# A two-layer hybrid decoder trunk: the compressed branch's probabilities are split ahead of their transposes, and the instruction planner gets other costs and rules

## The chip, the core and the metric

The kernel runs on one core of a Trainium2 chip. The metric is the time of one execution on the device, in microseconds (us). Three executions of the kernel before are recorded: 586.84, 588.35 and 589.41 us, median 588.35. One more execution was taken with the hardware profiler; everything said of single instructions comes from it.

The engines go by short names: PE is the matrix engine (PEld its loading of stationary operands), DVE the vector engine, ACT the scalar engine, POOL the general engine, SP the queue that starts most transfers. Each engine works through its own instructions in the order in which they were written.

## The reference

Two layers, each on x of 512 tokens by 1024 columns in float32. One projection of x by `w_in` (3352 columns) feeds three mixers side by side; their outputs are gated, concatenated, projected by `w_out` and normalised. Cut to what matters here:

```
proj = x @ w_in            # split into rq rk rv rg nq nkc nvc nks nvs nkw nvw ng ngl lx lg
y_ret = retention(rq, rk, rv) * silu(rg)                 # 4 heads of 64, chunks of 128
y_nsa = nsa(nq, nkc, nvc, nks, nvs, nkw, nvw, ngl, ...) * silu(ng)
y_lru = rg_lru(lx, conv_w, conv_b, ...) * silu(lg)       # causal conv of width 4, then a gated recurrence
x = layer_norm(alpha * x + concat(y_ret, y_nsa, y_lru) @ w_out)

# nsa, 8 query heads in 2 groups:
kc = compress(nkc) ; vc = compress(nvc)     # 31 blocks of 32 tokens, stride 16: (block + pos) @ w
p_c = softmax(q kc^T, masked)               # 31 columns          -> o_c = p_c vc
p_s = softmax(q ks^T, causal)               # selected branch     -> o_s   (all 8 blocks fit, so: causal)
p_w = softmax(q kw^T, causal)               # window branch       -> o_w
out = g0 * o_c + g1 * o_s + g2 * o_w        # g = sigmoid(ngl)
```

## The kernel before

Float32 products are built from two parts: a value is split into `hi` (its rounding to the matrix engine's float32r format) and `lo` (the rest), and a product is hi·hi + hi·lo + lo·hi. So every chunk of weights is loaded (`wr`), rounded on ACT (`wh`) and its rest taken on POOL (`wl`), in four pieces of two 256-column slices each; x is kept transposed as `XH` and `XL`. The 13 column chunks of `w_in` are projected in the order of `CHUNKS` (nv, nk, nq0, cmp, nq1, lx, lg, rq, rk, rv, rg, ng0, ng1), then four chunks of `w_out`, for each of the two layers. Products go to eight PSUM banks: three for projections (`A`), two for scores (`S`), one each for transposes (`T`), for values (`O`) and for the rest (`M`).

The attention goes over token tiles of 128 in the order 1, 2, 0, 3 and over two groups of four heads. For a tile, group and branch: the scores in a bank S; DVE adds the mask and finds the maximum (the custom operation that writes `P` and `nmx`); ACT takes the exponential in place and its sum (`den`); `gate_rec` takes the reciprocal of `den` and multiplies by the branch's gate; `scale_row` scales each of the four heads' rows, heads 0 and 1 on POOL and 2 and 3 on DVE (`SCALE = "GGVV"`); in `values`, PE transposes four 128 by 128 blocks into bank T, ACT and DVE split them (`pth`, `ptl`), and two products add to bank O. There are 32 such branch groups and 80 transposed blocks in the two layers.

The compressed branch has 16 small softmaxes (one per tile and group, `pcm`, four heads by 31 columns). Before, `pcm` is transposed as one 128 by 128 block into bank T, and then the transposed block is split: four ACT copies of 32 rows and four DVE subtractions of 32 rows fill 64 rows of `pc` (high parts over low parts), and a product with 64 rows adds to bank O. Bank T is taken until the last of the eight has read it. The compressed keys and values come from `kt2`, which holds the projected columns in its upper 64 rows and the same, one token on, in its lower 64 (DVE copies), and from 16 pairs of products.

The order of the instructions is not the order of the source. Every call is recorded by `Engine.record` and becomes an `Op` with a cost in ns (`Engine.cost`), a lag to its users (`LAG`), a flag whether it holds the SBUF ports that DVE and POOL share (`Engine.locks`), and the buffers that it touches. `Plan.schedule` makes a list schedule: first by the longest path to the end plus a random term (`SEED`, `NOISE`), then six rounds of packing to the end and to the start; the best is written out. Nothing of this runs on the chip: the result is a fixed order per engine and the buffers' places. Line L204 of the profile is the one place where all recorded instructions are issued, and L232 that of the paired products.

Of the kernel before, what the change touches and what calls it, by code (L numbers as in the profile page):

```python
# [17 lines left out]
P = 128  # L18
# [17 lines left out]
# columns of w_in in the order in which they are projected  # L36
# [36 lines left out]
# columns of the table of constants  # L73
C_MASK, C_MASKC, C_ANY, C_COS, C_SIN, C_DQ, C_DQ2, C_DV, C_ID, C_TRI = (
# [37 lines left out]
COLD = 6827.0  # the array's clock is halved until then  # L112
TURN = 130.0  # between two engines' accesses to a bank
# [5 lines left out]
PCB = 1  # L119
# how a token tile's halves are normalised: on DVE; on ACT and DVE; on ACT, DVE and Pool  # L120
NORM = [["AG", "AG", "VV", "VV"], ["AG", "AG", "VV", "VV"]]
LOCKS = True
K_ORDER = [0, 1, 6, 7, 2, 3, 4, 5]
# [3 lines left out]
SCALE = "GGVV"  # L127
W_ENG = "GGGG"
SEED = 174
# [7 lines left out]
class Ref:  # L137
    """A view of a buffer whose place is known once the schedule is."""
# [26 lines left out]
class Slots:  # L165
    """Places of one kind; buffers take them in the order in which they are made."""
# [23 lines left out]
class Engine:  # L190
# [3 lines left out]
    def __getattr__(self, what):  # L194
        f = getattr(self.queue, what)

        def record(*args, **kw):
# [12 lines left out]
            self.plan.add(self.name, call, self.cost(what, args, kw), reads, writes, table, self.locks(what, args, kw))  # L210
# [3 lines left out]
    def locks(self, what, args, kw):  # L214
        """Whether an instruction holds the SBUF ports that DVE and Pool share."""
# [8 lines left out]
        if len(sbuf) > 1:  # L224
            return True
        return what in ("tensor_copy", "tensor_scalar", "memset") and len(sbuf) == len(big) and at(args[0]).space != PSUM

    def together(self, *products):
        """Matrix products that the array takes side by side, as one instruction of the plan."""
# [4 lines left out]
        cost = self.cost("matmul", products[0][:3], {}) + 102.0 * (len(products) - 1)  # L234
        self.plan.add(self.name, call, cost, [r for x in products for r in x[1:3]], [x[0] for x in products], None, False)

    def cost(self, what, args, kw):
        at = lambda x: x.view(0) if isinstance(x, Ref) else x
        size = lambda x: int(np.prod(x.shape[1:]))
        in_psum = lambda x: x.space == PSUM  # L240
        out = at(args[0])
        n = size(out)
        if self.name == "SP":
            return max(475.0, out.nbytes() / DMA_RATE)
        if self.name == "PE":
            if what == "transpose":
                return 0.86 * at(args[1]).shape[0]
# [5 lines left out]
        psum = any(in_psum(x) for x in src)  # L253
        if self.name == "ACT":
            aps = any(isinstance(kw.get(k), Ref) for k in ("bias", "scale"))
            return (52 if psum else 93) + 0.833 * n + 93 * aps + 93 * ("accum_out" in kw)
        n = max([n] + [size(x) for x in src])
        if self.name == "POOL":
            if kw.get("op") == ALU.pow:
                return 164.0 * n  # L260
            if what == "memset":
                return 60 + 0.5 * n
            return 230 + 0.863 * n if what == "tensor_scalar" else 58 + 2.28 * n
        if what == "reciprocal":
            return 60 + 6.3 * n
        if what in ("tensor_copy", "tensor_scalar", "memset") and not psum and not in_psum(out):
            return 67 + 0.521 * n + 62 * (len(src) - 1)
        return 70 + 1.042 * n + 62 * (what == "scalar_tensor_tensor" and len(src) > 2) + (8 if what == "tensor_tensor_reduce" else 0)


class Plan:
# [7 lines left out]
    def touched(self, ref):  # L279
        """The quarters of the partitions and the cells of GRAIN elements that a view touches, as bits."""  # L280
# [15 lines left out]
    def add(self, eng, call, cost, reads, writes, table, lock):  # L296
        op = Op(eng, call, cost, table, lock and LOCKS, len(self.ops))
        for r in reads:
# [12 lines left out]
        op.bufs = {r.buf for r in reads + writes}  # L311
        for b in op.bufs:
# [823 lines left out]
```

## Time and profile before

| | |
|---|---|
| three executions | 586.84, 588.35, 589.41 us |
| span of the profiled execution, first to last instruction | 586.1 us (no time of its own is recorded beside it; the median of the three is 2.2 us more) |
| PE busy | 564.7 us, 96% of the span, 3670 products |
| DVE busy | 415.7 us, 71% |
| ACT busy | 336.7 us, 57% |
| POOL busy | 294.6 us, 50% |
| transfers | 52.6 MB, 90 GB/s over the span |

Busy time is the union of an engine's instructions from start to end. A product's end is modelled and lies well behind the start of the next, so PE can be busy by this count while no new product starts. What matters for PE is the distance from start to start, and what it waited for.

### The profile page before, as it was taken

The page shows a single profiled execution, that of the slowest core. Times are in us where ns is not written, and L with a number is a line of the kernel's source. Part 1 is how long each engine was busy: PE and PEld are TensorE (multiplying, and loading weights), DVE is VectorE, ACT ScalarE, POOL GpSimd, SP SyncE. Part 2 cuts the span into 40 slices and gives each one's busy share as a digit, 9 for nine tenths or more (in the row PEclk, how much of TensorE's full clock was granted, in tenths as well). Part 3 has the DMA queues.
Part 4 walks back from the last instruction along what each step waited for, and adds up shares of the span by engine and source line. Part 5 has one row for each costly group of instructions (what it writes and reads, how often), then busy time and mean ns, then how long its engine had stood idle before and what let it go on. Part 6 is the DMA issues. An engine that isn't in the chain of part 4 may idle for free.

```text
span 586.1 us, 10490 instructions
## 1 busy us (share of the span) xinstructions
PE 564.7 (96%) x3670; PEld 498.3 (85%) x3670; DVE 415.7 (71%) x1237; ACT 336.7 (57%) x785; POOL 294.6 (50%) x349
## 2 busy tenths in 40 slices
PE   8999999999989999999989999999999999999994
PEld 8888867889878888899988888788899888788994
DVE  6663499889998776743793227798797888676247
ACT  6464477698666655722443456758985666564220
POOL 3655155335845255754483454432596514378532
PEclk9999999999999999999999999999999999999997
DMA  8733222110323044343362433120213202332403
GB/s 259 263 100 108 73 72 73 38 36 1 85 61 91 4 124 116 100 148 104 137 180 55 125 79 103 37 73 1 73 38 107 71 21 57 106 127 59 134 7 145
DMA packets 44069, 52.63 MB, mean 90 GB/s; under 512 B 2928, under 2 KB 36720, under 8 KB 44016
## 3 DMA queue, kind: packets, MB, share of 16 engines
q1 hardware_dynamic: 44016, 51.95, 29.8%
q8 instruction: 29, 0.48, 0.3%
q14 instruction: 24, 0.20, 0.1%
HBM read 47.75 MB, written 4.19 MB: 89 GB/s over the span
## 4 chain that ended last, share of the span: by engine, by line
PE 71%; DVE 14%; ACT 8%; issue 2%; DMA 2%; POOL 2%; SPq 0%; DVEq 0%; POOLq 0%; ACTq 0%
PE A L204 50%; PE T L204 6%; PE S L204 6%; PE O L204 4%; PE M L204 4%; DVE P L204 3%; ACT pc L204 2%; DVE pc L204 2%; DVE R L204 2%; ACT P L204 2%; DVE Y L204 2%; DMA wr<-in_w_in_dram 1%; DVE ptl L204 1%; ACT R L204 1%; PE M L232 1%
## 5 line engine op out<-in xcount | busy, mean ns | idle before, releaser
L204 POOL TENSOR_TENSOR wl<-wr,wh 128x512 fp32r<-128x512 f32 (+2 forms) x136 | 180.6, 1343 | 111.5 <-ACT wh L204 93.0
L204 PE MATMUL A<-wh,XL 128*128 128x256 f32 (+1 forms) x560 | 155.3, 288 | 0.7 <-DVE XL L204 0.7
L204 PE MATMUL A<-wh,XH 128*128 128x256 f32 (+1 forms) x560 | 154.1, 288 | 1.1 <-ACT wh L204 1.1
L204 PE MATMUL A<-wl,XH 128*128 128x256 f32 (+1 forms) x560 | 153.6, 285 | 0.0
L204 ACT ACTIVATE wh<-wr 128x512 fp32r<-128x512 f32 (+2 forms) x140 | 82.0, 613 | 65.9 <-PE A L204 40.7
L204 PEld LDWEIGHTS A<-wh,XL 128*128 128x128 f32 x560 | 104.3, 190 | 3.6 <-issue 1.0
L204 PEld LDWEIGHTS A<-wh,XH 128*128 128x128 f32 x560 | 103.6, 189 | 4.0 <-ACT wh L204 1.4
L204 PEld LDWEIGHTS A<-wl,XH 128*128 128x128 f32 x560 | 104.1, 189 | 1.7 <-issue 0.2
L204 PE MATMUL A<-XH,wl 128*128 128x512 f32 x256 | 101.3, 405 | 0.0
L204 PE MATMUL A<-XL,wh 128*128 128x512 f32 x256 | 100.4, 401 | 0.0
L204 PE MATMUL A<-XH,wh 128*128 128x512 f32 x256 | 100.2, 401 | 0.0
L204 ACT ACTIVATE P<-P,nmx 128x128 f32<-128x128 f32 (+3 forms) x128 | 71.0, 556 | 36.4 <-DVE nmx L204 36.0
L204 DVE TENSOR_TENSOR ptl<-T,pth 128x512 fp32r<-128x512 f32 x80 | 55.0, 687 | 26.9 <-ACT pth L204 24.6
L204 ACT ACTIVATE pth<-T 128x512 fp32r<-128x512 f32 x80 | 47.5, 594 | 39.6 <-PE T L204 35.0
L204 DVE CUSTOM_DVE_ANT_0 P<-S,con 128x128 f32<-128x128 f32 (+3 forms) x128 | 60.0, 483 | 12.6 <-PE S L204 9.1
L204 POOL TENSOR_SCALAR P<-P,den 128x256 f32<-128x256 f32 (+3 forms) x64 | 38.9, 619 | 57.8 <-DVE denc L204 22.1
L204 PE MATMUL T<-con,P 128*128 128x128 f32 x320 | 58.5, 276 | 6.3 <-DVE pc L204 2.9
L204 PE MATMUL S<-K,Q 128*128 128x288 f32 (+4 forms) x240 | 61.0, 340 | 1.2 <-DVE nmx L204 1.0
L204 PEld LDWEIGHTS A<-XL,wh 128*128 128x128 f32 x256 | 48.2, 188 | 9.5 <-issue 0.2
L204 PEld LDWEIGHTS A<-XH,wl 128*128 128x128 f32 x256 | 48.2, 189 | 9.4 <-issue 0.9
L204 PEld LDWEIGHTS A<-XH,wh 128*128 128x128 f32 x256 | 48.3, 189 | 9.2 <-issue 0.7
L204 PEld LDWEIGHTS T<-con,P 128*128 128x128 f32 x320 | 39.6, 140 | 18.0 <-issue 4.4
(156 smaller groups left out, 899.4 us busy)
## 6 DMA issues: line engine op xcount, KB each, us to landing
wr<-in_w_in_dram SPq DMA_DIRECT2D x48, 512.0 KB, 3.8
wr<-in_w_out_dram SPq DMA_DIRECT2D x16, 512.0 KB, 3.9
Y<-in_xt_dram SPq DMA_DIRECT2D x8, 256.0 KB, 4.1
Y<-in_cmpw_dram SPq DMA_DIRECT2D x4, 512.0 KB, 6.1
R<-in_xn_dram SPq DMA_DIRECT2D x8, 256.0 KB, 3.4
P<-in_gb_dram SPq DMA_DIRECT2D x8, 256.0 KB, 3.9
x<-R SPq DMA_DIRECT2D x8, 256.0 KB, 2.0
R<-x SPq DMA_DIRECT2D x8, 256.0 KB, 3.1
```

What stands on the lines that cost most here:

```text
L204: return f(*[at(x) for x in args], **{k: at(v) for k, v in kw.items()})
L232: self.queue.matmul(out.view(), lhsT.view(), rhs.view(), **kw)
```

## The change

1. **Compressed branch.** `softmax_cmp` splits `pcm` itself, before any transpose: one ACT copy and one DVE subtraction over 128 rows give `pc2`, high and low parts of a head side by side. Four products with an identity in float32r (`idr`) then put the transposed 64 rows of each head into bank T, and a single ACT copy of 64 by 512 moves them to `pc`. `pc` and `vcs` have 128 rows now, the lower 64 zeroed once on POOL, so the product into bank O has 128 rows. `pcm`, `pc2` and `pc` have one buffer each (`pcm` had two).
2. **Scaling.** `gate` is multiplied by 0.25 where it is made. `scale_row` gets the reciprocal and the gate as two per-row operands, so the 32 multiplications of `den` by the gate fall away. `SCALE` is `"GGGV"`: three heads on POOL, one on DVE.
3. **wl pieces.** A `wl` piece of two slices becomes two of one slice (`W_CUT = 2`): 256 POOL instructions of 128x256 in place of 128 of 128x512 (and eight of 280 in place of four of 560).
4. **Shifted columns.** The lower half of `kt2` is filled by a transfer from SBUF to SBUF on SP's queue (two a layer) and not by eight DVE copies. The 16 pairs of products for the compressed keys and values are one entry of the plan, and so stand in a run.
5. **Other forms.** The low keys of the other half are a second subtraction from PSUM and not a DVE copy in SBUF. The convolution of the recurrent mixer reads the projection's bank four times (one ACT instruction with a scale and a bias, three DVE multiply-adds) and needs no shifted copy in SBUF.
6. **Start.** The first two slices of the weights are started from ACT's queue (`W_ACT = 2`), and the table of constants is loaded in two parts, the identity apart.
7. **Planner.** Costs and rules are other: a product costs 0.4465 ns a column plus 4 (0.4219 before); an instruction of ACT or DVE whose first row differs from that of the one before it in the same memory starts `HELD` = 115 ns later; the ports are kept per engine; transfers count as such on every queue; POOL is asked first; `SEED` is 12.

The core of the diff:

```diff
-SCALE = "GGVV"
+SCALE = "GGGV"
+W_CUT = 2
+W_ACT = 2
+HELD = 115.0
+POOL_EARLY = 60.0
-SEED = 174
+SEED = 12
...
     def cost(self, what, args, kw):
...
             if at(args[2]).dtype == F32R:
-                return max(0.4219 * n, 0.835 * m)
-            return 1.676 * max(n, m)
+                return max(0.4465 * n + 4.0, 0.86 * m)
+            return max(1.8 * n, 1.73 * m)
...
+    @staticmethod
+    def held(op, rows):
+
+        return HELD if any(rows[op.eng].get(k, v) != v for k, v in op.rows.items()) else 0.0
...
-                    t = max(op.known, at, free[e], ports if op.lock else 0.0)
+                    t = max(op.known, at, free[e] + self.held(op, rows), ports[e] if op.lock else 0.0)
...
-            ports = op.end if op.lock else ports
+            if op.lock and op.eng == "POOL":
+                ports["DVE"] = op.end - POOL_EARLY
+            elif op.lock:
+                ports["POOL"] = op.end
...
-                        Q.dma_start(raw[:, u, :], s3[:, r, :][:, u, :])
+                        (A if 4 * h + k < W_ACT else Q).dma_start(raw[:, u, :], s3[:, r, :][:, u, :])
...
-                        (G if W_ENG[2 * h + q] == "G" else V).tensor_sub(lo[:, u], raw[:, u], hi.bitcast(F32)[:, u])
+                        for v in range(2 * q, 2 * q + 2, 2 // W_CUT):
+                            u = slice(v, v + 2 // W_CUT)
+                            (G if W_ENG[2 * h + q] == "G" else V).tensor_sub(lo[:, u], raw[:, u], hi.bitcast(F32)[:, u])
...
-                V.tensor_copy(kst[ot, g, 1, c], kf[me, g, 1, c])
+                V.tensor_sub(at(ot, 1, kst), src, at(me, 0, kf))
...
-                V.tensor_copy(kt2[i][HD:, S * g:S * g + S - 1], kt2[i][0:HD, S * g + 1:S * g + S])
                 G.memset(kt2[i][HD:, S * g + S - 1:S * g + S], 0.0)
+            k2 = kt2[i][:, :2 * S].rearrange("p (g t) -> p g t", g=2)
+            Q.dma_start(k2[HD:, :, :S - 1], k2[0:HD, :, 1:])
...
-                lx = sb([P, S + 4], "R", 8)[:, :S + 3]
-                G.memset(lx[:, 0:3], 0.0)
-                A.activation(lx[:, 3:], ps, AF.Copy)
-                xc = sb([P, S + 4], "R", 8)[:, :S]
-                V.tensor_scalar(xc, lx[:, 0:S], lp[:, c, 0:1], lp[:, c, 4:5], op0=ALU.mult, op1=ALU.add)
-                for k in range(1, 4):
-                    V.scalar_tensor_tensor(xc, lx[:, k:k + S], lp[:, c, k:k + 1], xc, op0=ALU.mult, op1=ALU.add)
+                xc = sb([P, S], "R", 8)
+                A.activation(xc, ps, AF.Identity, scale=lp[:, c, 3:4], bias=lp[:, c, 4:5])
+                for k in range(2, -1, -1):
+                    V.scalar_tensor_tensor(xc[:, 3 - k:], ps[:, :S - 3 + k], lp[:, c, k:k + 1], xc[:, 3 - k:],
+                                           op0=ALU.mult, op1=ALU.add)
...
-                (G if eng == "G" else V).tensor_scalar(p_, p_, by, 1.0, op0=ALU.mult, op1=ALU.mult)
+                (G if eng == "G" else V).tensor_scalar(p_, p_, rec, gt, op0=ALU.mult, op1=ALU.mult)
...
             G.tensor_tensor(pm, pm, d[:, :, None].to_broadcast([P, 4, N_CMP]), op=ALU.mult)
+            two = sb([P, 4, 2, 32], "pc2", 1, F32R)
+            split(two[:, :, 0, :], two[:, :, 1, :], pcm)
+            return two
...
                 pt = bank("T")
-                T.transpose(pt[:, :P], pcm.rearrange("p r n -> p (r n)"), ident)
-                pc = sb([P, 4, P], "pc", PCB, F32R)
                 for r in range(4):
-                    A.activation(pc[0:32, r, :], pt[32 * r:32 * r + 32, :P], AF.Copy)
-                for r in range(4):
-                    V.tensor_sub(pc[32:64, r, :], pt[32 * r:32 * r + 32, :P], pc.bitcast(F32)[0:32, r, :])
-                T.matmul(po, vcs[0:64, g, :], pc[0:64].rearrange("p r t -> p (r t)"), start=False, stop=last)
+                    T.matmul(pt[0:64, r * P:r * P + P], pcm[:, r].rearrange("p e n -> p (e n)"), identr, start=True, stop=True)
+                A.activation(pc[0:64].rearrange("p r t -> p (r t)"), pt[0:64], AF.Copy)
+                T.matmul(po, vcs[:, g, :], pc.rearrange("p r t -> p (r t)"), start=False, stop=last)
```

Three places show how the rows move; the numbers behind the names are buffers.

On PE, the first compressed block of layer 1, from its transpose to its product. Before (`pcm` is the block, `T_70` the bank, `pc` the split block, `O_117` the output):

```order
L204 MATMUL T_70<-con_65,pcm_126 128x128
L204 MATMUL O_117<-pth_139,vst_74 128x512
L204 MATMUL A_87<-XH_71,wl_82 128x512
...
L204 MATMUL A_87<-XL_72,wh_79 128x512
L204 MATMUL A_87<-XH_71,wl_83 128x512
L204 MATMUL T_70<-con_65,P_132 128x128
L204 MATMUL T_70<-con_65,P_133 128x128
L204 MATMUL T_70<-con_65,P_134 128x128
L204 MATMUL T_70<-con_65,P_128 128x128
L204 MATMUL O_117<-pc_143,vcs_113 128x512
```

Now (`pc_0_140` is the split block, `T_79` the bank, `pc_80` its copy, `O_119` the output):

```order
L208 MATMUL T_79<-idr_66,pc_0_140 64x128 x4
L208 MATMUL A_97<-XH_81,wh_91 128x512
L208 MATMUL A_97<-XL_82,wh_91 128x512
L208 MATMUL A_97<-XH_81,wl_95 128x512
L208 MATMUL A_97<-XH_81,wh_91 128x512
L208 MATMUL S_100<-K_113,Q_114 128x384 x2
L208 MATMUL T_79<-idr_66,P_133 128x128
...
L208 MATMUL A_97<-XH_81,wh_89 128x512
L208 MATMUL O_119<-pc_80,vcs_115 128x512
```

One transpose has become four products of 64 columns; between them and the next use of bank T stand six other products now, and thirteen stood there before.

On POOL, in the attention of layer 1, a branch group of tile 2 (`den` the sums, `P` the rows to be scaled, `wl` the rests of the weights). Before:

```order
L204 TENSOR_TENSOR wl_84<-wr_76,wh_80 128x2x256 x2
L204 TENSOR_SCALAR P_133<-P_133,den_119 128x384
L204 TENSOR_SCALAR P_134<-P_134,den_119 128x384
L204 TENSOR_TENSOR pcm_126<-pcm_126,denc_137 128x4x31
L204 TENSOR_TENSOR wl_85<-wr_77,wh_81 128x2x256 x2
```

Now:

```order
L208 TENSOR_TENSOR wl_92<-wr_87,wh_88 128x256 x2
L208 TENSOR_TENSOR R_71<-rt_150 128x4x32
L208 TENSOR_SCALAR P_135<-P_135,den_123,gate_85 128x384
L208 TENSOR_SCALAR P_129<-P_129,den_123,gate_85 128x384
L208 TENSOR_SCALAR P_130<-P_130,den_123,gate_85 128x384
```

A group has three scalings in a row on POOL in place of two, and the pieces of `wl` around them are half as wide.

On SP, the first transfers (`Y` holds x until it is split, `wr` the raw weights). Before:

```order
L204 DMA Y_73<-in_xt_dram 128x512 x2
L204 DMA wr_76<-in_w_in_dram 128x280 x2
L204 DMA Y_73<-in_xt_dram 128x512 x3
...
L204 DMA Y_73<-in_xt_dram 128x512
L204 DMA lp_101<-in_lrup_dram 128x16
L204 DMA wr_76<-in_w_in_dram 128x4x256
```

Now:

```order
L208 DMA Y_83<-in_xt_dram 128x512 x2
L208 DMA wr_86<-in_w_in_dram 128x280 x2
L208 DMA Y_83<-in_xt_dram 128x512 x4
L208 DMA wr_87<-in_w_in_dram 128x280
L208 DMA Y_83<-in_xt_dram 128x512
L208 DMA wr_86<-in_w_in_dram 128x4x256
L208 DMA wr_87<-in_w_in_dram 128x280 x3
```

The first two slices of the weights have gone to ACT's queue, where they stand ahead of everything else, and the first half of the next chunk (`wr_86`, 128x4x256) stands ahead of the last three slices of the first chunk.

More of the change, by code (lines that the diff above doesn't have):

```diff
@@ L244, in cost @@
             return max(475.0, out.nbytes() / DMA_RATE)
+        if what == "dma_start":
+            return 475.0
         if self.name == "PE":
             if what == "transpose":
-                return 0.86 * at(args[1]).shape[0]
+                return 0.87 * at(args[1]).shape[0]
             m = size(at(args[1]))
             if at(args[2]).dtype == F32R:
-                return max(0.4219 * n, 0.835 * m)
-            return 1.676 * max(n, m)
+                return max(0.4465 * n + 4.0, 0.86 * m)
+            return max(1.8 * n, 1.73 * m)
         src = [at(x) for x in args[1:] if isinstance(x, Ref)]
         psum = any(in_psum(x) for x in src)
+        moved = any(row(x) != row(out) for x in src)
         if self.name == "ACT":
             aps = any(isinstance(kw.get(k), Ref) for k in ("bias", "scale"))
-            return (52 if psum else 93) + 0.833 * n + 93 * aps + 93 * ("accum_out" in kw)
+            some = psum and src[0].shape[0] < P
+            return (52 if psum else 93) + 0.833 * n + 93 * aps + 93 * ("accum_out" in kw) + 16 * moved + ACT_SOME * some
         n = max([n] + [size(x) for x in src])
@@ L311, in add @@
         op.bufs = {r.buf for r in reads + writes}
+        op.rows = {}
+        if eng in ("ACT", "DVE") and not dma:
+            for kind, refs in (("W", writes[:1]), ("R", reads)):
+                for r in refs:
+                    ap = r.view(0)
+                    op.rows.setdefault((kind, ap.space == PSUM), ap.offset // ap.ap[0][0])
         for b in op.bufs:
@@ L352, in forward @@
         free = dict.fromkeys(self.ENGINES, BEGIN)
-        table, ports = "exp", 0.0
+        table, ports = "exp", {"POOL": 0.0, "DVE": 0.0}
+        rows = {"ACT": {}, "DVE": {}}
         for op in self.ops:
@@ L371, in forward @@
             best = None
-            for e in self.ENGINES:
+            for e in ("POOL", "PE", "DVE", "ACT", "SP"):
                 pick = None
@@ L481, in bank @@
         return sb([P, 512], tag, BANKS[tag], where=psum)
-    con = sb([P, C_N], "con")
-    Q.dma_start(con, const_d)
-    ident = con[:, C_ID:C_ID + P]
+    con = sb([P, C_ID], "con")
+    Q.dma_start(con, const_d[:, :C_ID])
+    identr = sb([P, P], "idr", 1, F32R)
+    ident = identr.bitcast(F32)
+    ones = sb([P, S], "R", 8)[:, :P]
+    Q.dma_start(ones, const_d[:, C_ID:])
+    A.activation(identr, ones, AF.Copy)
     mhalf = sb([P, 4], "mhalf")
@@ L912, in scores @@
             probs = {b: [] for b in branches}
-            pcm = sb([P, 4, 32], "pcm", 2) if 0 in branches else None
+            pcm = sb([P, 4, 32], "pcm", 1) if 0 in branches else None
             if pcm is not None:
@@ L1028, in hybrid_kernel @@
         for i in TOKS:
-            xr[i] = [sb([P, S + 4], "R", 8)[:, :S] for _ in range(2)]
+            xr[i] = [sb([P, S], "R", 8) for _ in range(2)]
             for h in range(2):
```

85 lines of the change are left out of this document (52 added, 33 removed).

## The prediction

> **What bounds the kernel now.** I read the page's busy times first, then the chain that ended last, then what PE and its loads waited for, then the groups of instructions, and last the timeline around the longest waits.
>
> ```profile
> span 586.1 us, 10490 instructions
> PE 564.7 (96%) x3670; PEld 498.3 (85%) x3670; DVE 415.7 (71%) x1237; ACT 336.7 (57%) x785; POOL 294.6 (50%) x349
> PE 71%; DVE 14%; ACT 8%; issue 2%; DMA 2%; POOL 2%; SPq 0%; DVEq 0%; POOLq 0%; ACTq 0%
> ...
> 531.94 40.05 PE A L204 x336
> ```
>
> PE bounds it. Where nothing is late, as in the last row, a piece of the chain, a 128x256 product follows the other every 119 to 120 ns (40.05 us / 336). The rest of the chain, a quarter, is DVE and ACT: places where PE stood behind them. What PE and its loads waited for:
>
> ```profile
> PE T L204 <- DVE pc L204: 2.9, 8, 0.9
> PE T L204 <- DVE P L204: 2.6, 4, 0.9
> PE S L204 <- DVE nmx L204: 1.0, 2, 0.6
> PE O L204 <- DVE pc L204: 0.8, 2, 0.6
> PEld T L204 <- issue: 5.2, 13, 1.1
> PEld T L204 <- DVE P L204: 3.8, 5, 1.1
> PEld A L204 <- issue: 3.8, 16, 0.2
> PEld S L204 <- DVE nmx L204: 2.2, 4, 0.9
> PEld T L204 <- DVE ptl L204: 1.6, 3, 0.7
> ```
>
> The waits of the loads are longer, because a product's modelled end covers some 0.16 us of each (a 128x256 product is 0.28 us long and starts 0.12 behind the other). So the whole prize is some ten to thirty us, and only what moves these rows or PE's own work counts. Cheaper instructions on DVE, ACT or POOL are worth what PE waited for them.
>
> **The change part by part.** *Compressed products on PE: +2.0 us.* What a block costs PE now:
>
> ```profile
> 166.14 0.63 PE L204 MATMUL S<-K,Q 128*128 128x512 f32 x2
> 166.70 0.50 PE L204 MATMUL O<-pc,vcs 64*128 64x512 f32 x1
> 167.14 0.50 PE L204 MATMUL A<-wh,XL 128*128 128x256 f32 x2
> ...
> 58.16 0.40 PE L204 MATMUL A<-XH,wl 128*128 128x512 f32 x1
> 58.40 0.40 PE L204 MATMUL A<-XL,wh 128*128 128x512 f32 x1
> 58.73 0.31 PE L232 MATMUL M<-Y 128*64 128x65 f32 x1
> 58.73 0.30 PE L232 MATMUL T<-Y 128*64 128x65 f32 x1
> 58.85 0.30 PE L232 MATMUL M<-Y 128*64 128x65 f32 x1
> ```
>
> The two 512-wide scores and the 64-row product take 166.14 to 167.14, 1.00 us for three products of 512 columns; at 0.24 each (58.16 to 58.40) they would take 0.72. So 64 rows cost 0.28 more, going in and coming out, and that falls away with 128 rows: 16 x 0.28 = -4.5. The four new products have 64 columns of the array like `M<-Y`. Going into that form cost 58.73 - 58.40 = 0.33 for a product of 0.24, so 0.09; I take as much coming out. One product of it costs 0.06 (two start in each 0.12) to 0.11 if they don't go two and two, as the four here, on one place of the array, may not. So a block costs 0.18 + 4 x 0.06 = 0.42 to 0.18 + 4 x 0.11 = 0.62 and saves one transpose of 0.11: +0.31 to +0.51, times 16 is +5.0 to +8.2. With the -4.5 the sum is +0.5 to +3.7; the middle, +2.0.
>
> The Trainium skill ("TensorE: Matmul & The Clock Gate", "Why this matters for your kernels") says that one product over 32 rows takes the time of one over 128. By it the padding would bring nothing, and the sum would be 4.5 us higher. The trace does not agree: 0.28 us a product.
>
> *Compressed chain off bank T: -3.0 us.*
>
> ```profile
> L204 ACT ACTIVATE pc<-T x64: 250/269/275, 87.8 to 529.2; 32x128 fp32r<-32x128 f32 x64
> L204 DVE TENSOR_TENSOR pc<-T,pc x64: 279/285/295, 89.1 to 531.0; 32x128 fp32r<-32x128 f32 x64
> L204 ACT ACTIVATE pth<-T 128x512 fp32r<-128x512 f32 x80 | 47.5, 594 | 39.6 <-PE T L204 35.0
> ```
>
> Bank T is held by four times 269 and four times 285 ns, 2.2 us a block; then by one ACT copy as long as `pth<-T`, 0.6. The order shows six products before the bank's next use, 4 x 0.24 + 2 x 0.18 (384 columns) = 1.3 us, which covers that copy with its hand-overs, and would not have covered 2.2. So the 2.9 and 0.8 us of the rows on `pc` go, up to 3.7; I take 3.0, since with one buffer of `pcm`, `pc2` and `pc` some block will be late.
>
> *DVE held by POOL: -4.5 us.*
>
> ```profile
> 164.90 0.33 PE L204 MATMUL T<-con,P 128*128 128x128 f32 x1 [0.90 <-DVE P L204]
> 162.25 2.60 DVE L204 TENSOR_SCALAR P<-P,den 128x128 f32<-128x128 f32 x2
> 162.27 2.49 POOL L204 TENSOR_TENSOR wl<-wr,wh 128x512 fp32r<-128x512 f32 x2 [0.78 <-ACT wh L204]
> ```
>
> Two scalings took 2.60, as long as the two `wl` pieces beside them, and PE stood 0.90 us for the second. Shorter pieces halve such a hold; one scaling on DVE in place of two halves their number; the multiplications of `den` fall away. What PE waited for DVE's `P`, `nmx` and `ptl` is 3.8 + 2.2 + 1.6 = 7.6 us on the loads, 3.6 of it (`P` and `nmx`) on the products. Bounds: 0 and -7.6; I take -4.5.
>
> *Three scalings on POOL, more pieces: +2.0 us.*
>
> ```profile
> L204 POOL TENSOR_TENSOR wl<-wr,wh 128x512 fp32r<-128x512 f32 x128 | 170.1, 1344 | 103.0 <-ACT wh L204 84.5 <-PE A L204 7.9 <-issue 2.6
> L204 POOL TENSOR_TENSOR ryn<-ryn,R 128x256 f32<-128x256 f32 x8 | 6.2, 776 | 13.9 <-DVE ryn L204 12.4 <-DVE R L204 1.5
> L204 POOL TENSOR_SCALAR P<-P,den 128x256 f32<-128x256 f32 (+3 forms) x64 | 38.9, 619 | 57.8 <-DVE denc L204 22.1
> ```
>
> Two pieces of 256 cost 2 x 776 - 1344 = 0.21 us more than one of 512: 128 x 0.21 = 27 us of POOL at most; 32 more scalings at 0.62 (the row's mean) are 19.8. POOL goes from 295 to about 340 of 586 us, and its idle time covers that. Not covered is the third scaling of a group: it ends 0.62 later than the second did, and the transposes need all four rows. There are 32 groups; 32 x 0.62 = 19.8 is the upper bound, 0 the lower. PE has projections to do in most places (four and five waits on `P` in the rows above), so I charge three to four groups: +2.0.
>
> *Start: -0.7 us.*
>
> ```profile
> 1.63 0.90 SPq L204 DMA_DIRECT2D wr<-in_w_in_dram  x2
> 6.32 0.83 PE L204 MATMUL A<-wh,XH 128*128 128x280 f32 x2 [1.07 <-ACT wh L204]
> 9.51 0.40 PE L204 MATMUL S<-wl,XH 128*128 128x280 f32 x1
> 9.74 0.30 PE L204 MATMUL S<-wh,XL 128*128 128x280 f32 x1
> 9.88 0.29 PE L204 MATMUL A<-wl,XH 128*128 128x280 f32 x1
> ```
>
> The weights were issued at 1.63; ACT's queue can at about 0.7, so the first product's wait of 1.07 goes. But until 9.74 products start every 0.23 us and only then every 0.13, so a start 1.1 us sooner brings five products that later cost 0.13 each: 0.7. Against it: SP now waits with the next chunk's first half until `wr_86` is free, and three slices of the first chunk stand behind that. Range -1.5 to +1.5.
>
> *Covered edits: 0.* The shift by transfer is issued when ACT has written the four parts and is needed by the run of pairs. In the order 24 products of 512 (5.8 us in layer 1) and 22 (5.3 us) stand between, against two ACT copies, the issue, and a landing like the one of 256 KB below:
>
> ```profile
> 53.43 2.30 ACT L204 ACTIVATE Y<-A 64x512 f32<-64x512 f32 x4
> R<-x SPq DMA_DIRECT2D x8, 256.0 KB, 3.1
> ```
>
> That is 1.2 + 0.4 + 3.1 = 4.7; without the cover it would be as much, twice. On SP's queue the weights of lx stand behind it, and a whole chunk (nq1) is projected before those are needed. The key subtraction and the convolution take DVE out of SBUF-to-SBUF forms and hold bank A longer (three multiply-adds, some 2 us); two other banks A cover that.
>
> *The new order: -3.5 us.* The planner counted a 512-wide product 0.4219 x 512 = 216 ns and counts 233 now; the timeline above has 0.24. It also knows holds that it did not. Lower bound: the waits of the loads that no other part takes, `issue` on T and A, 5.2 + 3.8 = 9 us. Upper bound, from two of the 40 us stretches between 60 and 540 (the first number after the stretch is its length, the next PE's busy time):
>
> ```profile
> 140.00:180.00 40.00, 37.05 (x268) 32.95 (x266) 37.60 (x138) 25.47 (x76) 26.46 (x35) 1.00 0.20 54
> 460.00:500.00 40.00, 39.76 (x273) 35.32 (x273) 33.09 (x117) 25.56 (x64) 18.19 (x20) 1.00 0.23 67
> ```
>
> PE stood 2.95 us in the worse and 0.24 in the better; four more stretches like the worse are +12. I lean to the lower side because the counted cost now meets the measured one: two fifths of the bound.
>
> **Sum:** 2.0 - 3.0 - 4.5 + 2.0 - 0.7 - 3.5 = -7.7 us. The span 586.1 becomes 578.4; the median of the runs lies 2.2 above the span, so 580.6 us, 1.3% less. Less than 0.5% (2.9 us) cannot be told from no change.
>
> **Rivals.** *No change, 587.* The waits only change their names: bank T comes free, and the next thing PE needs (the scaled rows, a bank S) is late by as much. For it: on T, the waits on `issue` and on DVE are mixed already. Against: bank T is freed 1.6 us sooner in 16 places without another user. Price: the -4.5 and -3.5 do not come: 588.35 + 2.0 - 3.0 + 2.0 - 0.7 = 588.6; with a part of them, 587.
>
> *POOL late, 597.* The third scaling stands behind `wl` pieces and transposes wait for it in most groups. For it: SP waited for POOL's `wl` more than for anything else, so POOL's queue is already what frees the raw buffers; against: POOL is idle half of the time, and 0.62 us is five projections of 256 columns. If every group is exposed, 588.35 - 7.7 - 2.0 + 19.8 = 598.5; it is slower than before by 0.5% from 0.62 us in 21 of 32 groups on ((7.7 + 2.0 + 2.9)/0.62). I give 597.
>
> ```profile
> SPq L204 <- POOL wl L204: 339.6, 59, 26.7
> ```
>
> The Trainium skill speaks for this rival ("SBUF — State Buffer", "Who interferes with whom"): a DVE instruction with two SBUF inputs, or a two-port form, and a POOL instruction exclude each other for the whole instruction, whichever comes first. More instructions on POOL then mean more holds. The row of 2.60 us agrees.
>
> *Twice the gain, 572.* The waits on DVE vanish whole and the new order takes its 9 us: 588.35 + 2.0 - 3.7 - 7.6 - 0.7 - 9.0 = 569.4, and 572 with most of it. For it: stretches of 40 us without any wait exist. Against: it needs all at once.
>
> **How the numbers follow.** Forecast (575 to 585) 0.56, twice the gain 0.12, no change 0.18, POOL late 0.14. The first two are faster: 0.68; same 0.18; slower 0.14. The likeliest's own range is 575 to 585; for 8 in 10 I reach to 569, where the gain would be all the waits, and to 591, where the no-change case ends.
>
> **What would show it.** The 64-row product's distance of 0.44 becomes 0.23, and the four `T<-idr,pc` take 0.4 to 0.6 us. No PE wait on `pc` over 1 us in sum. DVE scalings beside `wl` last at most one short piece. PE's waits on POOL `P` stay under 3 us. The first product with weights starts before 5.5. The prediction is wrong if PE's waits on POOL grow past 8 us, if the run of pairs waits for its transfer, or if waits on `issue` and DVE in sum are what they were.

## The result, and the profile after

The changed kernel takes **577.44 us** (median of 4 runs, 576.45 to 578.28) against 588.28 for the kernel before: a ratio of **0.9826 (95% interval 0.9803 to 0.9849)**, 10.8 us less between the medians and 1.7% less by the ratio. The profiled execution took 577.81 us, 1.8 above its span. The page of the profile after, its span, busy times and shares of the chain of waits:

```profile
span 576.0 us, 10627 instructions
...
PE 559.9 (97%) x3718; PEld 500.6 (87%) x3718; DVE 373.8 (65%) x1113; ACT 331.6 (58%) x754; POOL 336.5 (58%) x512
...
PE 76%; DVE 9%; ACT 7%; DMA 4%; POOL 2%; issue 2%; DVEq 0%; POOLq 0%; ACTq 0%; SPq 0%
```

PE is the bound as before, and more of the chain is its own: 76% against 71, with DVE at 9% against 14. From the start of the first product to that of the last it is 566.2 us (576.3 before); what lies behind that start is 8.7 us (8.8 before). So all of the gain is on PE, and the view of waits tells what kind of time it was. Of the changed kernel, the rows that answer to those shown of before, with the largest new ones (us in sum, times, longest):

```profile
PE A L208 <- ACT wh L208: 1.6, 1, 1.6
PE T L208 <- DVE P L208: 1.5, 2, 1.3
...
PE S L208 <- DVE nmx L208: 0.3, 1, 0.3
...
PEld T L208 <- DVE ptl L208: 2.7, 9, 0.6
PEld A L208 <- ACT wh L208: 2.0, 2, 1.8
PEld T L208 <- DVE P L208: 2.0, 2, 1.5
...
PEld S L208 <- DVE nmx L208: 0.8, 2, 0.6
```

The rows on `pc` are gone (2.9 and 0.8 us before). So are nearly all on `issue`: 2.3 us in sum on the loads, 11.9 before. Summed over all rows of the view, PE's products waited 7.0 us (12.1 before) and the loads 19.6 (31.8), 9.3 of it for DVE (13.1). The stretch 140 to 180, in which PE had stood 2.95 us, is full. Over the twelve stretches of 40 us from 60 to 540 PE stands for 4.7 us, where it had stood for 10.8; the worst two are now the last two here (length, then PE's busy time):

```profile
140.00:180.00 40.00, 39.87 (x296) 37.16 (x295) 37.01 (x146) 30.02 (x84) 32.20 (x56) 1.00 0.23 59
...
260.00:300.00 40.00, 38.30 (x309) 37.17 (x309) 26.59 (x52) 15.77 (x30) 26.60 (x32) 1.00 0.39 123
...
420.00:460.00 40.00, 38.46 (x283) 35.55 (x282) 36.52 (x134) 25.46 (x75) 27.26 (x49) 1.00 0.19 54
```

PE's timeline around one block's compressed branch, and the instructions of the tile `pc` (shortest, median, longest in ns):

```profile
89.10 0.39 PE L208 MATMUL O<-pth,vst 128*128 128x512 f32 x1
89.33 0.40 PE L208 MATMUL T<-idr,pc 128*64 128x128 f32 x4
89.57 0.44 PE L208 MATMUL A<-XH,wh 128*128 128x512 f32 x1
...
93.09 0.39 PE L208 MATMUL A<-XH,wh 128*128 128x512 f32 x1
93.32 0.39 PE L208 MATMUL O<-pc,vcs 128*128 128x512 f32 x1
93.55 0.40 PE L208 MATMUL A<-XL,wh 128*128 128x512 f32 x1
```

```profile
L208 PE MATMUL T<-idr,pc x64: 220/223/303, 89.3 to 520.7; 128*64 128x128 f32 x64
L208 ACT ACTIVATE pc<-T x16: 572/592/598, 89.9 to 521.5; 64x512 fp32r<-64x512 f32 x16
```

The product of 128 rows takes its 0.23 us and nothing beside it. Four `T<-idr,pc` take 0.24 us together (89.33 to 89.57), and the 512-wide product ahead of them keeps its usual 0.23 (89.10 to 89.33): there is no price for going into 64 columns or out of them.

### The profile page after: what moved, and what is told of

It is laid out like the page before. It is cut to its first block, busy times and chain, and to the rows that moved or that the text cites. A ratio compares the mean times of both kernels' runs of the same rounds, so it can differ in the third digit from the quotient of the medians.

```text
span 576.0 us, 10627 instructions
## 1 busy us (share of the span) xinstructions
PE 559.9 (97%) x3718; PEld 500.6 (87%) x3718; DVE 373.8 (65%) x1113; ACT 331.6 (58%) x754; POOL 336.5 (58%) x512
## 4 chain that ended last, share of the span: by engine, by line
PE 76%; DVE 9%; ACT 7%; DMA 4%; POOL 2%; issue 2%; DVEq 0%; POOLq 0%; ACTq 0%; SPq 0%
PE A L208 52%; PE T L208 6%; PE O L208 6%; PE S L208 5%; PE M L208 5%; DMA wr<-in_w_in_dram 3%; DVE R L208 2%; DVE P L208 2%; ACT P L208 1%; DVE Y L208 1%; ACT wh L208 1%; PE M L239 1%; DMA lp<-in_lrup_dram 1%; ACT pth L208 1%; POOL wl L208 1%
## 5 line engine op out<-in xcount | busy, mean ns | idle before, releaser
L208 POOL TENSOR_TENSOR wl<-wr,wh 128x256 fp32r<-128x256 f32 (+1 forms) x268 | 199.1, 771 | 114.1 <-ACT wh L208 107.2
L208 PE MATMUL A<-wh,XL 128*128 128x256 f32 (+1 forms) x560 | 153.5, 285 | 0.3 <-DVE XL L208 0.2
L208 PE MATMUL A<-XH,wl 128*128 128x512 f32 x256 | 100.1, 400 | 0.0
L208 PE MATMUL A<-XL,wh 128*128 128x512 f32 x256 | 99.2, 397 | 0.0
L208 POOL TENSOR_SCALAR P<-P,den,gate 128x256 f32<-128x256 f32 (+3 forms) x96 | 61.2, 651 | 40.8 <-DVE den L208 38.5
L208 ACT ACTIVATE P<-P,nmx 128x512 f32<-128x512 f32 (+3 forms) x128 | 70.8, 555 | 13.0 <-DVE nmx L208 12.7
L208 DVE CUSTOM_DVE_ANT_0 P<-S,con 128x512 f32<-128x512 f32 (+3 forms) x128 | 59.6, 484 | 12.9 <-PE S L208 7.4
L208 PE MATMUL T<-idr,P 128*128 128x128 f32 x320 | 53.9, 275 | 1.9 <-DVE P L208 1.5
L208 PEld LDWEIGHTS T<-idr,P 128*128 128x128 f32 x320 | 38.4, 141 | 9.0 <-DVE P L208 2.0
```

Of the source, the lines that this page charges most:

```text
L208: return f(*[at(x) for x in args], **{k: at(v) for k, v in kw.items()})
```

## The experiments

Theory: the gain is time in which PE stood, taken away by a shorter compressed chain first and by shorter holds of DVE second; PE's own work is nearly unchanged. Rivals: it is one lucky order of instructions; it is the planner's new costs; it is the ports alone.

The runs are of two kinds. In the first, the order is that of the changed kernel, instruction for instruction, and one thing is exchanged in it when the instructions are written out. In the second, the program is planned anew, with the first of the seeds 0 to 59 by the planner's end unless the text says another. All are compared with runs of the kernel before on the same chip; the table has every one.

| Run | us | Ratio to before (95%) |
|---|---|---|
| changed kernel again | 576.74 | 0.9817 (0.9799 to 0.9836) |
| products over 64 rows, same order | 583.27 | 0.9920 (0.9902 to 0.9939) |
| `wl` pieces of 512, same order | 582.62 | 0.9913 (0.9899 to 0.9928) |
| third scaling on DVE, same order | 580.24 | 0.9876 (0.9860 to 0.9892) |
| eight parts out of bank T, same order | 595.94 | 1.0138 (1.0120 to 1.0156) |
| before's instructions, new planner | 599.94 | 1.0210 (1.0178 to 1.0242) |
| changed instructions, old planner | 579.02 | 0.9848 (0.9830 to 0.9865) |
| changed kernel, second seed | 585.35 | 0.9958 (0.9942 to 0.9973) |
| changed kernel, middle seed | 592.07 | 1.0060 (1.0034 to 1.0086) |
| compressed branch as before, planned anew | 588.51 | 1.0025 (1.0000 to 1.0051) |
| pieces and scalings as before, planned anew | 581.40 | 0.9888 (0.9869 to 0.9907) |
| another seed, three more products of zeros | 573.95 | 0.9766 (0.9740 to 0.9791) |

### One thing exchanged in the changed kernel's order

**The measure**, the changed kernel once more:

> The changed kernel once more, as the measure for the three runs beside it, which have its order of instructions with one thing exchanged. 577.4 us, as it had; more than 1.5 us away would say that these comparisons can't carry 2 us.

576.74 us, 0.7 from the first. The two profiled executions differ at the start, of which more below.

**Rows.**

```diff
-T.matmul(po, vcs[:, g, :], pc.rearrange(...), ...)
+T.matmul(po, vcs[0:64, g, :], pc[0:64].rearrange(...), ...)
```

> The changed kernel in its own order, with the sixteen products of the compressed probabilities over 64 rows in place of 128 (the added rows are zeros, so the result is the same). My term: a product over 64 rows among products over 128 costs 0.28 us more, 16 x 0.28 = +4.5 us, and the product's distance to the next goes from 0.23 to 0.42 or more. By the rule that rows don't matter (the Trainium skill, "TensorE: Matmul & The Clock Gate", "Why this matters for your kernels") the time is the same to within 0.5 us.

583.27, so +6.5 us. PE's timeline of this run, at the block shown above:

```profile
92.98 0.39 PE L208 MATMUL A<-XH,wh 128*128 128x512 f32 x1
93.30 0.49 PE L1024 MATMUL O<-pc,vcs 64*128 64x512 f32 x1
93.72 0.50 PE L208 MATMUL A<-XL,wh 128*128 128x512 f32 x1
```

0.32 going in and 0.42 coming out, in place of twice 0.23: 0.28 us a product, 4.5 in sixteen, as forecast. The Trainium skill ("TensorE: Matmul & The Clock Gate", "Why this matters for your kernels") has one product over 32 rows take the time of one over 128; for products over 64 rows among products over 128 this trace does not agree. Of the other 2 us the products' waits show 1.2 (8.2 us in place of 7.0). The loads' waits on `issue` came back with the rows, 8.9 us in place of 3.0.

**Pieces of `wl`.**

```diff
-for v in range(2 * q, 2 * q + 2, 2 // W_CUT):
-    u = slice(v, v + 2 // W_CUT)
-    G.tensor_sub(lo[:, u], raw[:, u], hi[:, u])
+u = slice(2 * q, 2 * q + 2)
+G.tensor_sub(lo[:, u], raw[:, u], hi[:, u])
```

> The changed kernel in its own order, with each pair of wl pieces of 256 again as one subtraction of 512, at the place of the first of the two. My theory (shorter pieces halve the time for which DVE is held): POOL's busy time falls by some 18 us (the pieces took 180.6 us before and 199.1 after), DVE's single scalings last up to 1.4 us and more, PE's waits for DVE's P and ptl (3.5 and 2.7 us on PE and its loads) grow by half, and the time rises by 1 to 4 us. The rival (the pieces' size is of no account, POOL's time is): the time is the same or falls by up to 2 us.

582.62, so +5.9, more than expected, although POOL is busy for 314.6 us in place of 336.7. The loads' waits for DVE grow from 9.2 us (the changed kernel again) to 14.0; the largest rows:

```profile
PEld T L208 <- DVE ptl L208: 4.0, 12, 1.0
PEld A L208 <- DVE XL L208: 2.9, 7, 0.7
```

`ptl` had 2.8 us in the changed kernel again. The time for which POOL is busy counts for nothing here, and the length of one of its instructions for a lot; part of the 5.9 may be that the order was made for the short pieces. Of the two rows that I had named, `ptl` grew by nearly half, but the loads' wait for `P` fell, from 2.0 to 1.0 us.

**Third scaling.**

(of the four rows of a group, the third)

```diff
-G.tensor_scalar(p_, p_, rec, gt, ...)
+V.tensor_scalar(p_, p_, rec, gt, ...)
```

> The changed kernel in its own order, with the third scaling of each group issued on DVE at the same place in place of POOL. My theory (the scalings on DVE are what PE waits for, since wl pieces hold them): DVE's busy time rises by 32 x 0.6 = 19 us, PE's waits for DVE's P grow from 1.5 us to 4 or more, and the time rises by 2 to 5 us. The rival (the third scaling on POOL is late, as my term of +2.0 and the case POOL late have it): the time falls by 2 us, and PE's waits for POOL's P vanish.

580.24, so +3.5: the size of the theory and the opposite of the rival. The mechanism was not the one expected. PE's products wait 0.5 us for DVE's `P`, not 4. These are the largest of the rows that grew, and the place of the first of them:

```profile
PE A L208 <- POOL wl L208: 1.5, 1, 1.5
...
PEld A L208 <- POOL wl L208: 2.6, 4, 1.8
PEld S L208 <- DVE nmx L208: 2.2, 6, 0.6
```

```profile
17.96 0.40 PE L208 MATMUL A<-wl,XH 128*128 128x280 f32 x1 [1.55 <-POOL wl L208]
```

The waits for `wl` are not the exchange's. The longest lies at 17.96 us, and the first scaling of this run starts at 77.4; and POOL's pieces of 256 take 764 ns on average here, 767 in the changed kernel again. What is left is `nmx`, 2.2 us on the loads where it was 0.8: DVE, busy for 382.3 us in place of 372.6, is later with its maxima. That this is all of the 3.5 is not shown. In this order the third scaling on POOL is not a cost, it is a gain.

**Eight parts out of bank T.**

```diff
-A.activation(pc[0:64], pt[0:64], AF.Copy)
+for r in range(4):
+    A.activation(pc[0:32, r, :], pt[0:32, r * P:r * P + P], AF.Copy)
+for r in range(4):
+    V.scalar_tensor_tensor(pc[32:64, r, :], pc[0:32, r, :], 0.0, pt[32:64, r * P:r * P + P], op0=ALU.mult, op1=ALU.add)
```

> The changed kernel in its own order, with the one ACT copy of a block's compressed probabilities out of bank T replaced by four copies on ACT and then four multiply-adds on DVE, of 32 rows each, each of which waits for the copies, as before the change. My term: the bank is held by 8 x 0.27 = 2.2 us in place of 0.6, six products cover 1.3 us, and the time rises by 3.0 (up to 3.7) us, with waits for DVE's pc on PE. DVE has 16 x 4 x 0.28 = 18 us more in this order than it was made for, which may add 1 to 2. The rival (PE has other work while bank T is held): less than 1 us, and no wait on pc.

595.94, so +19.2, six times the term. The view of PE's waits has the direct part; the timeline has one of the ten places, the second longest:

```profile
PE T L208 <- DVE pc L1028: 8.6, 10, 1.2
```

```profile
130.20 0.40 PE L208 MATMUL T<-idr,pc 128*64 128x128 f32 x4
...
132.56 0.72 ACT L1026 ACTIVATE pc<-T 32x128 fp32r<-32x128 f32 x4
133.31 0.88 DVE L1028 SCALAR_TENSOR_TENSOR pc<-pc,T 32x128 fp32r<-32x128 f32 x4 [1.24 <-ACT pc L1026]
...
134.34 0.63 PE L208 MATMUL T<-idr,P 128*128 128x128 f32 x4 [1.20 <-DVE pc L1028]
```

The eight instructions themselves take 0.72 and 0.88 us (they overlap), less than my 2.2. But ACT came to them 2 us late, DVE stood 1.24 us for ACT, and the bank was held for 4 us, with PE behind it. From the first compressed product of a block to the end of its last copy out of the bank it is 2.4 us in the median of the sixteen blocks, against 1.4 in the changed kernel again (and 2.8 in the kernel before, from the transpose on). The loads' waits double, 38.9 us against 19.9: 6.4 us of them are now for POOL's `P` (0.7 there) and 5.1 are on `issue` for T (0.3). How much of the 19.2 is the chain and how much an order that was made without it, this run cannot say. The next kind says more, but has the choice of the order in it.

### Planned anew

**The compressed branch undone alone.**

```diff
-two = sb([P, 4, 2, 32], "pc2", 1, F32R)
-split(two[:, :, 0, :], two[:, :, 1, :], pcm)
...
-T.matmul(pt[0:64, r * P:r * P + P], pcm[:, r], identr, start=True, stop=True)
-A.activation(pc[0:64], pt[0:64], AF.Copy)
-T.matmul(po, vcs[:, g, :], pc, ...)
+T.transpose(pt[:, :P], pcm, ident)
+A.activation(pc[0:32, r, :], pt[32 * r:32 * r + 32, :P], AF.Copy)
+V.tensor_sub(pc[32:64, r, :], pt[32 * r:32 * r + 32, :P], pc[0:32, r, :])
+T.matmul(po, vcs[0:64, g, :], pc[0:64], ...)
```

> The changed kernel with the compressed branch alone as it was before (one transpose, eight parts out of bank T, products over 64 rows), planned anew, with the first of seeds 0 to 59 by the planner's end (50), as 12 is for the changed kernel. From the runs so far: the rows were worth 6.5 us when undone in the old order; the four products cost the changed kernel 64 x 61 ns = 3.9 us, less the transposes' 16 x 0.11 = 1.8. Theory: 577 + 4.5 - 2.1 + 3.0 = 582, since a planner that knows the chain's length can put work behind it. Rival (all of the gain is the compressed branch): 587 or more. Second rival (the branch is worth nothing once the order is made for it): 578 or less.

588.51 (its executions spread from 587 to 596): the time of the kernel before, so the first rival's number came out. What PE waited for in it:

```profile
PE S L208 <- DVE pcm L208: 3.8, 1, 3.8
...
PEld A L208 <- issue: 4.5, 17, 0.8
```

No product waits for `pc`: a planner that knows the chain puts work behind it. The loads wait for 28.3 us against 19.6, 9.3 of it on `issue` against 2.3. But the 3.8 us for `pcm` have a cause of their own (DVE, POOL, then a stretch with the granted clock third from the end):

```profile
453.94 5.50 DVE L208 TENSOR_SCALAR P<-P,den,gate 128x128 f32<-128x128 f32 x1
```

```profile
453.83 5.53 POOL L208 TENSOR_TENSOR wl<-wr,wh 128x256 fp32r<-128x256 f32 x8
```

```profile
460.00:464.00 4.00, 3.99 (x19) 3.80 (x20) 3.46 (x20) 0.31 (x1) 0.39 (x2) 0.60 0.82 246
```

One scaling on DVE lasted as long as eight `wl` pieces in a row on POOL, the operation on `pcm` stood behind it on DVE, and after the wait the mean granted clock of a stretch of 4 us is 0.60, which costs up to (1 - 0.60) x 4 = 1.6 us. So up to 3.8 + 1.6 = 5.4 of the 11 us lie in this one place, in a hold of DVE by POOL that the order happens to have, and not in the compressed branch. The run bounds what the branch is worth; it does not measure it.

**Pieces and scalings undone alone.**

```diff
-SCALE = "GGGV"
+SCALE = "GGVV"
-W_CUT = 2
+W_CUT = 1
```

> The changed kernel with wl pieces of 512 and two scalings on POOL and two on DVE, as before, and all else as changed, planned anew with the first of seeds 0 to 59 (48). In the changed kernel's own order the two edits were worth 5.9 and 3.5 us when undone one at a time. Theory (the compressed branch carries the gain, as the run with that branch alone undone says, and an order made for them absorbs the ports): 577 to 582. Rival (the short pieces and the third scaling carry most of it themselves): 584 to 589.

581.40, so the two are worth 4.0 us together (4.7 against the changed kernel again) where each cost 3.5 and 5.9 in an order made for the change. Of the 4.0, 1.6 lie between the first and the last product (567.8 us against 566.2); 2.0 lie behind the last one, where neither a piece nor a scaling stands.

**The planner alone, the instructions alone.** Before's program with the changed planner, and the changed program with before's:

> The kernel before, its instructions untouched, with the changed planner (its costs, held instructions and ports) and, of the seeds 0 to 59, the one whose order the planner itself ends first. My term: the new order alone brings -3.5 us, between -9 and +12; PE's waits (issue, P, nmx) fall. The first rival: the gain needs the changed instructions, and the order alone gives 588, within 2 us. A second rival: an order for new costs on instructions that hold each other for 1.3 us is worse, +3 us or more.

> The changed kernel's instructions with the planner of before (its costs, one common hold for DVE and POOL, nothing on held instructions), and the best of seeds 0 to 59 by that planner. My terms without the order: -7.7 + 3.5 = -4.2 us, so 584. If all of the gain is the instructions': 577 to 579. If they need the planner (POOL has 17% more work whose holds the old planner prices with other numbers): 588 or more.

599.94 and 579.02. The order alone is slower than the kernel before by 11.7 us; the instructions alone, in an order by the old planner, bring 9.2 us. The new planner adds 1.6. Each of these numbers is of one order. What happened in one of the two worst places of the order alone: PE's rows, and three stretches of 4 us (length, PE's busy time, then its loads, DVE, ACT and POOL; the granted clock is the third number from the end):

```profile
130.09 0.50 PE L207 MATMUL O<-pth,vst 128*128 128x512 f32 x1 [0.96 <-ACT pth L207]
...
131.95 0.71 PE L207 MATMUL S<-K,Q 128*128 128x416 f32 x1 [0.51 <-DVE nmx L207]
```

```profile
128.00:132.00 4.00, 2.52 (x11) 1.41 (x10) 3.49 (x12) 4.00 (x11) 3.81 (x5) 0.99 0.00 0
132.00:136.00 4.00, 3.60 (x11) 2.30 (x11) 2.59 (x7) 3.55 (x7) 2.73 (x4) 0.50 0.54 153
136.00:140.00 4.00, 4.00 (x14) 2.76 (x13) 3.30 (x13) 3.14 (x7) 0.00 (x0) 0.66 0.37 109
```

PE stood 1.48 of 4 us, and for the next 7 its clock was halved. In the other place, 418 to 422, PE is busy for 1.23 of 4 us, and the clock of the next 4 is 0.57. So a cluster of waits is paid twice. The mean granted clock of this run is 0.987: (1 - 0.987) x 598 = 7.8 us at most went to the halved clock. Of these, 2.6 lie behind the last product, where no product stands; there the 2.9 of the kernel before, (1 - 0.995) x 586, lie too.

**Seeds.**

> The changed kernel with seed 52, the second of seeds 0 to 59. Theory: between the changed kernel and the middle seed, 577 to 581. Rival (one lucky order): 584 or more.

> The changed kernel with seed 33, the middle one of seeds 0 to 59 by the planner's end, in place of 12, which is its first. How much of the gain is the choice of the seed: my theory says that waits of the order as a whole count, so 579 to 584, the gain halved at worst. The rival (the gain is one lucky order): 586 or more. If the seed were of no account: 577, within 1 us.

585.35 and 592.07, against 577.4 for seed 12: the same instructions, 15 us apart, and the middle seed is slower than the kernel before. Both expectations of the theory were missed, on the side of the rival. The chosen seed is part of the gain, and with 8 us between the first seed and the second no difference of a few us between two planned kernels is shown to be that of their parts. It doesn't follow that the gain is luck: the kernel before has a chosen seed too, and other orders of the changed instructions keep it (579.02 above, and the last run):

```diff
-SEED = 12
-NOISE = 300.0
+SEED = 824
+NOISE = 1000.0
+for i in range(3):
+    T.queue.matmul(zt[:, :P], kz[:, 0, 0, :], kz[:, 0, 0, :], start=False, stop=False)
```

> The changed kernel with seed 824 at three times the noise, the first by the planner's end among some 1100 orders, and three more products of zeros at the start, which fill part of the 1.65 us in which PE stands before the first product with weights. The spread of the seeds so far (577, 585, 592 in the order of the planner's end) says that an order ranked ahead of 12 gives 573 to 577. Rival (the ranks say nothing so near the top): 578 to 585. In the first 20 us: if the clock is lost to the idle time, products start every 0.13 us from 7 us on in place of 10; if not, as before.

**573.95 us, ratio 0.9766 (0.9740 to 0.9791)**: faster than both kernels. PE's products wait 3.9 us in all. Its start, and that of the changed kernel ahead of it:

```profile
6.16 0.53 PE L208 MATMUL A<-wh,XH 128*128 128x280 f32 x2 [1.65 <-ACT wh L208]
...
7.50 0.43 PE L208 MATMUL A<-wl,XH 128*128 128x280 f32 x1
```

```profile
5.75 0.46 PE L208 MATMUL A<-wh,XH 128*128 128x280 f32 x1
...
7.77 0.29 PE L208 MATMUL A<-wl,XH 128*128 128x280 f32 x1
7.90 0.29 PE L208 MATMUL S<-wl,XH 128*128 128x280 f32 x1
```

In the changed kernel the products after the wait of 1.65 us soon take 0.43 each, until 10.8; here they take 0.29 and follow each other every 0.13 us from 7.8 on. By 20 us 91 products with weights have started in place of 87. That the filling did either is not shown. The run with the third scaling on DVE has the changed kernel's start, unfilled; it waited 0.97 us, kept the fast rate from its first product on, and had started 86 by 20 us. The run with pieces and scalings as before had the slow rate until 9.2, and had started 91. The gain over the changed kernel is, as far as these runs tell, the order.

## Why the prediction was right, and where it was not

580.6 was forecast, 577.4 measured, inside the likeliest case's own range (575 to 585). The span fell by 10.1 us where the sum had 7.7, and most of it, 6.1, is time in which PE had stood between 60 and 540. That the number is so near is in part luck: two terms have the wrong sign, one failed, one is not shown, and the errors cancel in part. Point by point:

- *Compressed products on PE, +2.0: mis-sized, and of the wrong sign.* The 64-row products were right: -4.5. The four new products are 0.24 us a block less one transpose of 0.11, or 16 x 0.13 = +2.1, not +5.0 to +8.2. The sum is -2.4. The step that failed is "Going into that form cost 58.73 - 58.40 = 0.33 for a product of 0.24, so 0.09; I take as much coming out." The 0.09 was read at the run of pairs, whose first load also stood 0.37 us for its issue; at `T<-idr,pc`, with nothing to wait for, entry and exit cost nothing. The pairing that was in doubt makes no difference either, the four start every 0.06 us.
- *Compressed chain off bank T, -3.0: right mechanism, the size is open.* The rows on `pc` are gone, 3.7 us. The bank is held for 1.4 us a block in place of 2.8 (the medians above), where I had 0.6 and 2.2: the bank is held not only for its users' durations but also while each engine comes round to its part, and I had left that out on both sides. Undone in the fixed order, the wait of PE alone is 8.6 us in ten of sixteen places, and the time 19.2. Undone and planned anew, the run is 588.5 - 577.4 = 11.1 us slower (11.8 against the changed kernel again), up to 5.4 of it in the hold that has nothing to do with the branch; less the 2.4 of its products, 3.3 or more are left for the chain and for what one order is better than another by. These runs don't tell the two apart.
- *DVE held by POOL, -4.5, and three scalings and more pieces, +2.0: near in sum, the second of the wrong sign.* Together -2.5; planned anew the two edits measure 4.0, of which 1.6 lie where PE works. The loads' waits for `P`, `nmx` and `ptl` fell from 7.6 to 5.5 us and not by 4.5, and that for `ptl` rose, from 1.6 to 2.7. In the changed kernel's order the third scaling on POOL is a gain, and POOL's busy time rose to 336.5 (340 forecast) with little wait of PE for it: 0.7 us of the loads for its `P`. So the rival POOL late fell. That scalings on DVE last at most one short piece was wrong, as the next section shows.
- *Start, -0.7: failed.* ACT's queue does bring the first weights sooner, their copy starts at 4.73 in place of 5.83. But on ACT a part of x comes next (5.08 to 5.69) and then the copy of the second slice (5.67 to 6.11), and PE's wait for ACT's `wh` ended behind that: the first product started at 6.16 (5.57 in the changed kernel again), not before 5.5. The slow rate lasted until 10.8, where before it had ended at 9.7; in the changed kernel again it ended at 9.4. By 20 us 87 products had started in both, 90 before: a loss of about half a us.
- *Covered edits, 0: right to half a us in this order.* In the changed kernel again the run of pairs waited 0.5 us for its transfer, which the prediction names as a sign that it is wrong; in the first, its loads waited 0.7 us on `issue` in both layers together. It isn't covered in every order: in the one by the old planner the run of pairs stood 2.4 us on `issue`, and the clock was 0.50 in the 3 us behind it.
- *The new order, -3.5: not shown.* With the changed instructions the new planner measures -1.6, with those of before +11.7, and the seeds spread over 15 us. The step that failed is that a counted cost which meets the measured one makes a better order: the order for before's instructions was worse by its own waits. A term for a new order should have had bounds of that size. Its lower bound of 9 us failed too, because other terms had taken many of these waits already. Two places of the kernel before (each the load, then a product):

```profile
132.42 0.20 PEld L204 LDWEIGHTS T<-con,P 128*128 128x128 f32 x2 [1.09 <-issue]
132.45 0.41 PE L204 MATMUL T<-con,P 128*128 128x128 f32 x2 [0.77 <-DVE pc L204]
...
166.70 0.50 PE L204 MATMUL O<-pc,vcs 64*128 64x512 f32 x1
167.13 0.30 PEld L204 LDWEIGHTS A<-wh,XL 128*128 128x128 f32 x2 [0.25 <-issue]
```

The largest wait on `issue` for T and four more, 2.7 of the 5.2 us, are at products that wait for `pc` themselves, the -3.0; and nearly all of those for A stand behind a 64-row product, some 0.25 us each, the -4.5. The runs agree: with the eight parts back there are 5.1 us on `issue` for T (5.2 before the change), and with the 64 rows back 2.8 us for A (3.8).

The rival *no change* had the waits only change their names. Against it is that PE stands for 4.7 us between 60 and 540, where it had stood for 10.8. *Twice the gain* did not come about in this order; the last run, in another order, is 14.0 us below the kernel before on its chip.

What is shown is that the gain is for the most part time in which PE had stood, with 2.4 us of its products, and that each part costs when it is undone in the changed kernel's order. How the gain divides among the parts and the order is open: undone one by one there, rows, pieces, scaling and copy come to 35.1 us, over three times the gain.

## What to carry to other kernels

A part undone in a fixed order is priced together with the misfit of that order, so undo it in both ways, and compare planned kernels only at the same depth of search: here the seed moved the time by more than the change did. A buffer that several engines empty in turn is held for their queues' delays as well as for their instructions: 2.8 us here where the durations gave 2.2, and 1.4 with a single copy of 0.6. Before two waits are priced as two, look whether they stand at the same time. Before a run that undoes a part is taken for its price, look where its longest wait comes from. Where the compute engine stands for long, look at its clock behind the wait as well as at the wait.

## What was not expected of the hardware

**A hold goes from one POOL instruction to the next.** PE's longest wait behind the start, 1.34 us, is for a scaling on DVE of 128 x 128, 316 ns at its fastest, that lasted 2.45 us (DVE's timeline, then POOL's):

```profile
440.82 2.45 DVE L208 TENSOR_SCALAR P<-P,den,gate 128x128 f32<-128x128 f32 x1
```

```profile
440.08 1.31 POOL L208 TENSOR_SCALAR P<-P,den,gate 128x128 f32<-128x128 f32 x3
441.36 0.47 POOL L208 TENSOR_TENSOR R<-rt 128x128 f32<-128x128 f32 x1
441.77 1.42 POOL L208 TENSOR_TENSOR wl<-wr,wh 128x256 fp32r<-128x256 f32 x2
```

POOL had instructions ready one after the other, and DVE's ended only with the last of them, at 443.27, having stood beside parts of five. It came again at 441.4 in the changed kernel again (2.44 us), and with the compressed branch undone and planned anew eight pieces in a row held one scaling for 5.50 us (above). So cutting a piece in two doesn't bound the hold where nothing stands between the pieces. The Trainium skill ("SBUF — State Buffer", "Who interferes with whom") has a DVE instruction in a two-port mode and one of POOL exclude each other: whoever issues first gets the shared ports for the whole instruction. By that DVE, which stood ready beside the first of the five, should have had them before the second; these rows do not agree.

**The clock can fall on short waits.** 1.48 us of standing within 4, the longest wait of PE 0.96, were followed by half the clock for some 7 us (the rows of the order alone above), and 1.65 us at the start of the changed kernel by three. Not every such stretch does it: with the products over 64 rows PE stood 1.58 us between 290.04 and 293.45, and the clock stayed at 1.00. What decides is not shown. At the start the column is no guide: in the changed kernel again it says 1.00 from 4 to 9.5, while products start every 0.23 us until 9.4. The Trainium skill ("TensorE: Matmul & The Clock Gate", "Why this matters for your kernels") has drops avoided where no idle gap passes some 3 us; that did not hold here. Another section of that page ("A second HAM failure mode: psum-queue depth-cycling") tells of a clock that falls with frequent short idling, and with it these rows agree.
